# Products of P and values in two attention groups: column-tiled matmuls issued in larger runs

## The chip, the cores and the metric

The kernel runs on one core of a Trainium2 chip. The metric is the device time of one execution in microseconds (us). Times of runs are medians; the trace is one profiled execution.

## What is computed

The program is a two-layer backbone over 2048 latent tokens and 256 context tokens (2304 keys), width 1024. Each layer has four groups of heads that read one input projection, then one output projection. The change touches two groups:

```
# group A: 4 query heads, 2 key/value heads of width 64 (two query heads share one key/value head)
p = softmax(q @ k^T * 64**-0.5);  o = p @ v
# group B: 4 heads, two softmax maps over keys of width 32
p1 = softmax(q1 @ k1^T * 32**-0.5);  p2 = softmax(q2 @ k2^T * 32**-0.5)
o = (p1 - lam * p2) @ v;  then a norm per head
# group C: neighbourhood attention with bias, the same product p @ v with 6 or 7 key tiles
```

Group D is a state-space layer. Scores use a 32-bit type of reduced precision, and the products of P and values plain 32-bit floats, each of which the trace shows as two matmul records.

## The kernel before

Keys are cut into 18 tiles of 128 (16 latent, 2 context). Per layer the ten attention units run in the order of `UNITS` (a0, b0, a1, b1, c0, b2, c1, b3, c2, c3; `chain`, L1857). While one unit attends, the input projection of the next is woven into it as filler by `F.pe`, `F.act`, `F.dve` and `F.keys` (class `Fill`): one `F.pe(1)` puts a weight block's three matmuls (L377, L378, L379) there. The order on TensorE, ScalarE and VectorE is that of the code (`manual_schedule`); GpSimd and the DMA queues are ordered by the scheduler.

**Group A** (`attend_a`, L754). A unit is one key/value head with its two query heads. It goes over blocks of 512 queries (4, and one of 256 context queries in layer 0) and in each over the 18 key tiles x. `score(x)` (L873) puts the transposed scores of both query heads into one PSUM tile sx with four matmuls (L878, L879), and ScalarE's two exponentials (L881) write them as PT tiles. `value(x)` (L883) has two column-tiled matmuls (L886): the values are 128 keys by 64, so head 0 fills columns 0 to 63 of the array and head 1 columns 64 to 127, and both accumulate in one PSUM tile acc. `value` also adds PT into running sums (L897), on GpSimd for some tiles and on VectorE for the others. In step x the loop calls `value(x - 1)`. In between, `ahead` works out the row maxima of the next block in parts: a matmul L812 into sz or sy, a reduction L814 on VectorE. The last block of a unit has no next one, and filler may have run out.

**Group B** (`attend`, L954, `maps == 2`). A unit is one head, an iteration one tile of 128 queries, for i in three stages: scores (L1001) into sx, sz, sy of map 0 and map 1, maxima (L1045), exponentials (L1060), and for the tile before, the combined P (`combine`, L1084), its transposes (`trans`, L1100) in groups g = 0 to 4 of 4, 4, 4, 4 and 2 key tiles into one PSUM tile tr, `evac` (L1114) on ScalarE from tr to a PT tile, and `pv` (L1116) with one column-tiled matmul for each key tile (L1126): even key tiles on columns 0 to 63, odd ones on 64 to 127, the halves added later by `ysum` (L1137). There is one tr, so a `trans` waits for the `evac` of the group ahead of it. The order around the change, with filler left out:

```
first half:   pv 1 | scores map 1 part 0 | part 1 | evac 2, trans 3, evac 3 | part 2 | pv 2 | trans 4
              pv 3 | evac 4 | trans 0 of the next tile | pv 4
second half:  scores map 0 of the next tile, trans 1, ysum ... | pv 0 | trans 2
```

PT tiles come from a ring of 7, shared by the groups.

Of the kernel before, what the change touches and what calls it, by code (L numbers as in the profile page):

```python
# [9 lines left out]
F32 = mybir.dt.float32  # L10
# [148 lines left out]
class Net:  # L159
# [594 lines left out]
    def attend_a(self, l, G, F):  # L754
# [3 lines left out]
        nc, p = self.nc, self.ap  # L758
# [68 lines left out]
        def finish(ts, raw, tot):  # L827

            n = len(ts)
            rec = p.tile([128, 2, 4], F32, name="mxa")  # L830
            for h in range(2):
                lp = self.ps_tr(n * 128)
                for i in range(n):
                    nc.tensor.matmul(lp[:, i * 128:(i + 1) * 128], tot[:, h, i * 128:(i + 1) * 128], self.two,
                                     start=True, stop=True)
                nc.vector.reciprocal(rec[:, h, :n], lp.rearrange("p (n d) -> p n d", d=128)[:, :, 0])
                yield
            tr = self.ps_tr(n * 128)
            for i in range(n):
                nc.tensor.transpose(tr[:, i * 128:(i + 1) * 128], raw[:, 0, i * 128:(i + 1) * 128], self.ident)  # L840
            yo = raw[:, 1].rearrange("p (n d) -> p n d", d=128)
            for i in range(n):
                for h in range(2):
                    o = slice(h * 64, h * 64 + 64)
                    nc.vector.scalar_tensor_tensor(yo[:, i, o], tr[:, i * 128 + h * 64:i * 128 + h * 64 + 64],
                                                   rec[:, h, i:i + 1], gt[:, ts[i], o], op0=OP.mult, op1=OP.mult)
            for i, t in enumerate(ts):
                nc.sync.dma_start(self.y[l, t][:, G["col"]:G["col"] + 128], yo[:, i])
            yield
# [15 lines left out]
        for b, ts in enumerate(blocks):  # L865
            w = len(ts) * 128
            kts = list(range(NT)) if ts[0] < NLAT else [NLAT, NLAT + 1]
            n = len(kts)
            Q = Qs.pop(b)
            ahead = maxima(b + 1) if b + 1 < len(blocks) else iter(())  # L870
            sums, PTs, held = {}, {}, []

            def score(x):  # L873
                ks = slice(kts[x] * 128, kts[x] * 128 + 128)
                PTs[x] = [p.tile([128, 512], F32, name="PT", bufs=7) for _ in range(2)]
                o = self.ps_s(0, 1024)
                for h in range(2):
                    nc.tensor.matmul(o[:, h * 512:h * 512 + w], kst[:, ks], Q[0][:, h, :w], start=True, stop=False)  # L878
                    nc.tensor.matmul(o[:, h * 512:h * 512 + w], k2[0:65, ks], Q[1][0:65, h, :w], start=False, stop=True)  # L879
                for h in range(2):  # L880
                    nc.scalar.activation(PTs[x][h][:, :w], o[:, h * 512:h * 512 + w], AF.Exp, scale=0.125)  # L881

            def value(x):  # L883
                PT = PTs.pop(x)
                for h in range(2):
                    nc.tensor.matmul(acc[h * 64:(h + 1) * 64, :w], v[:, kts[x], :], PT[h][:, :w], start=(x == 0),  # L886
                                     stop=(x == n - 1))
                e = x // 2 if x < 4 else int(x % 3 == 2)
                if x in (0, 2):
                    held.append(PT)  # L890
                    return
                eng = nc.gpsimd if e else nc.vector
                if x in (1, 3):
                    sums[e] = p.tile([128, 2, 512], F32, name="Ta", bufs=3)
                for h in range(2):
                    first = held[e][h] if x in (1, 3) else sums[e][:, h]
                    eng.tensor_tensor(sums[e][:, h, :w], first[:, :w], PT[h][:, :w], op=OP.add)  # L897

            for x in range(n):
                F.t += 1  # L900
                score(x)
                if x % 4 == 2:
                    next(ahead, None)
                if x == 1:
                    acc = self.ps_acc()
                if 2 <= x <= 4:
                    next(done, None)
                if x:
                    value(x - 1)
                if x:  # L910
                    next(ahead, None)
                F.pe(1, 2)
                F.pe(1)
                if x:
                    next(ahead, None)
                F.act()
                if x % 2:
                    F.keys()
                if x % 2:
                    F.keys_copy()  # L920
                F.dve()
                yield True
            F.pe()
            value(n - 1)
            raw = p.tile([128, 2, 512], F32, name="Ta", bufs=3)
            nc.scalar.activation(raw[:, 0, :w], acc[:, :w], AF.Copy)
            for _ in done:
                F.pe(A_REST)
            for h in range(2 if n > 2 else 0):
                nc.vector.tensor_tensor(sums[0][:, h], sums[0][:, h], sums[1][:, h], op=OP.add)  # L930
            for _ in ahead:
                F.pe()
            done = finish(ts, raw, sums[0])
# [20 lines left out]
    def attend(self, l, G, F):  # L954


        nc, p = self.nc, self.ap
        kind, maps = G["kind"], G["maps"]
        steps = list(range(NT if l == 0 else NLAT))
        n = len(steps)  # L960
# [126 lines left out]
        def group(t, g):  # L1087
            kts = R[t, 0]["kts"]
            g0 = g * 4
            return kts[g0:g0 + 4], g0, len(kts)  # L1090
# [11 lines left out]
        def evac(t, g):  # L1102
            grp, g0, _ = group(t, g)
            if not grp:
                return
            r = R[t, 0]
            PT = r["PT", g] = p.tile([128, 4, 128], F32, name="PT", bufs=7)
            tr = r.pop(("tr", g))
            full = sum(1 for x in grp if x[2] == 128)
            spans = [(128, 0, full)] if full else []  # L1110
            if full < len(grp):
                spans.append((grp[-1][2], full, len(grp)))
            for w, x, y in spans:
                nc.scalar.activation(PT[:w, x:y], tr[:w, x * 128:y * 128].rearrange("p (a b) -> p a b", b=128), AF.Copy)  # L1114

# [43 lines left out]
        def at(i, f, *a):  # L1159
            if 0 <= i < n:  # L1160
                f(steps[i], *a)
# [5 lines left out]
        def half():  # L1167
            F.t += 1
            return True
# [10 lines left out]
        yield True  # L1180
        for i in range(n + (3 if maps == 2 else 2)):
            if maps == 2:
                at(i - 2, pv, 1)
                F.act()
                at(i, maxes, 0)
# [11 lines left out]
                if not early:  # L1197
                    at(i - 2, trans, 2)
                at(i - 2, evac, 2)
                at(i - 2, trans, 3)  # L1200
                at(i, exp, 0, 2)
                at(i - 2, evac, 3)
                at(i, scores, 1, 2)
                at(i - 2, pv, 2)
                at(i - 2, trans, 4)
                F.dve()
                F.pe(1)
                at(i - 3, finish)
                at(i, maxes, 1)
                at(i - 2, pv, 3)  # L1210
                F.act()
                F.pe(1)
                F.pe()
                F.act()
                early = i < n and not F.merged
                at(i - 2, evac, 4)
                F.act()
                if early:
                    at(i - 1, trans, 0)
                at(i - 2, pv, 4)  # L1220
                yield half()
                at(i, sums, 0)
                at(i, neg_max, 1)
# [26 lines left out]
                    F.keys(1)  # L1250
                    F.keys_copy()
                F.keys_copy()
                at(i - 1, pv, 0)
                early = i + 1 < n and not F.merged
                F.dve()
                if early:
# [747 lines left out]
```

## Time and profile before

| what | us |
|---|---|
| median of 3 runs (5153.1 to 5166.4) | 5156.62 |
| the profiled execution, its own time | 5158.76 |
| its span in the trace | 5156.9 |
| TensorE busy (matmuls) | 4681.1 (91%) |
| VectorE, ScalarE, GpSimd busy | 3215.5, 2568.4, 1912.5 |
| mean granted TensorE clock | 0.958 |

In the trace, PE is TensorE's matmuls, PEld its weight loads, DVE VectorE, ACT ScalarE, POOL GpSimd. A timeline row is a group of equal instructions: its start, the time to its end, engine, line, operation, out<-in, how many, and in brackets how long the engine was idle before it and what ended that. Matmuls are pipelined and their ends are modelled, so that rows overlap: what a group costs is read from one row's start to the start of the next. A "MATMUL ... x8" of L1126 is 4 key tiles.

### The profile page before, as it was taken

The page shows a single profiled execution, that of the slowest core. Times are in us where ns is not written, and L with a number is a line of the kernel's source. Part 1 is how long each engine was busy: PE and PEld are TensorE (multiplying, and loading weights), DVE is VectorE, ACT ScalarE, POOL GpSimd, SP SyncE. Part 2 cuts the span into 40 slices and gives each one's busy share as a digit, 9 for nine tenths or more (in the row PEclk, how much of TensorE's full clock was granted, in tenths as well). Part 3 has the DMA queues.
Part 4 walks back from the last instruction along what each step waited for, and adds up shares of the span by engine and source line. Part 5 has one row for each costly group of instructions (what it writes and reads, how often), then busy time and mean ns, then how long its engine had stood idle before and what let it go on. Part 6 is the DMA issues. An engine that isn't in the chain of part 4 may idle for free. (4 is left out here: it accounts for less than half of the span.)

```text
span 5156.9 us, 85866 instructions
## 1 busy us (share of the span) xinstructions
PE 4681.1 (91%) x31076; PEld 3585.3 (70%) x31076; DVE 3215.5 (62%) x7061; ACT 2568.4 (50%) x6522; POOL 1912.5 (37%) x3035
## 2 busy tenths in 40 slices
PE   7788998899999999998996879988999999999998
PEld 3686646665678777776676866566657777877777
DVE  8473767676674846724972737686767648476245
ACT  3332346634675856744341233466346658566431
POOL 4363443434233233321642534434342332333112
PEclk8899999999999999999998999999999999999999
DMA  7847212322235344253668573123223343433432
GB/s 255 287 151 202 88 41 66 98 95 72 91 121 167 103 144 132 83 178 116 194 213 281 169 198 109 49 65 98 95 72 98 111 152 100 155 122 117 130 134 107
DMA packets 360184, 677.66 MB, mean 131 GB/s; under 512 B 161872, under 2 KB 262224, under 8 KB 306768
## 3 DMA queue, kind: packets, MB, share of 16 engines
q0 software_dynamic: 54432, 396.39, 22.9%
q1 hardware_dynamic: 299280, 270.47, 17.9%
q10 hardware_dynamic: 6048, 5.31, 0.3%
q8 instruction: 247, 4.05, 0.3%
q14 instruction: 177, 1.45, 0.1%
HBM read 561.66 MB, written 110.36 MB: 130 GB/s over the span
## 5 line engine op out<-in xcount | busy, mean ns | idle before, releaser
L377 PE MATMUL pj<-WH,hs 128*128 128x256 f32 (+2 forms) x2592 | 814.9, 314 | 22.1 <-ACT b_v L733 7.1
L378 PE MATMUL pj<-WL,hs 128*128 128x256 f32 (+2 forms) x2592 | 753.3, 291 | 2.7 <-POOL WL L367 2.7
L379 PE MATMUL pj<-WH,hs 128*128 128x256 f32 (+2 forms) x2592 | 752.3, 290 | 0.0
L1114 ACT ACTIVATE PT<-tr 128x512 f32<-128x512 f32 (+1 forms) x788 | 440.5, 559 | 310.0 <-PE tr L1100 303.3
L377 PEld LDWEIGHTS pj<-WH,hs 128*128 128x128 f32 x2592 | 498.1, 192 | 125.3 <-issue 68.2
L388 POOL DMA_DIRECT2D hs<-hs x378 | 227.7, 603 | 956.0 <-PE pj L379 475.6
L378 PEld LDWEIGHTS pj<-WL,hs 128*128 128x128 f32 x2592 | 499.2, 193 | 26.6 <-POOL WL L367 3.3
L881 ACT ACTIVATE PT<-sx 128x512 f32<-128x512 f32 x584 | 315.3, 592 | 378.1 <-PE sx L879 367.6
L379 PEld LDWEIGHTS pj<-WH,hs 128*128 128x128 f32 x2592 | 497.7, 192 | 2.4 <-issue 2.4
L1045 DVE TENSOR_REDUCE sm<-sx 128x1 f32<-128x1024 f32 (+1 forms) x276 | 321.8, 1166 | 210.2 <-PE sx L1001 208.9
L1060 ACT ACTIVATE Ta<-sx,sm 128x1024 f32<-128x1024 f32 (+1 forms) x340 | 324.5, 955 | 108.2 <-DVE sm L1054 87.2
L886 PE MATMUL acc<-PT,a_v 128*64 128x512 f32 (+1 forms) x1168 | 315.8, 617 | 0.0
L897 POOL TENSOR_TENSOR Ta<-Ta,PT 128x512 f32<-128x512 f32 x160 | 219.5, 1389 | 204.4 <-ACT PT L881 203.9
L1126 PE MATMUL acc<-PT,b_v 128*64 128x128 f32 (+1 forms) x3200 | 277.9, 290 | 4.4 <-DVE sm L1073 1.5
L1001 PE MATMUL sx<-b_kst,qs 128*128 128x512 f32 (+2 forms) x618 | 218.3, 441 | 58.1 <-ACT Ta L1060 57.4
L814 DVE TENSOR_REDUCE mxa<-sy 128x1 f32<-128x1024 f32 (+1 forms) x256 | 209.8, 820 | 89.9 <-PE sy L812 86.8
L897 DVE TENSOR_TENSOR Ta<-Ta,PT 128x512 f32<-128x512 f32 x288 | 217.0, 794 | 77.0 <-ACT PT L881 76.5
L878 PE MATMUL sx<-Tb,a_kst 128*128 128x512 f32 x584 | 246.8, 423 | 19.5 <-ACT PT L881 19.5
L1100 PE MATMUL tr<-ident,Ta 128*128 128x128 f32 x1576 | 246.5, 278 | 13.9 <-ACT PT L1114 10.2
L1045 DVE TENSOR_REDUCE sm<-sy 128x1 f32<-128x768 f32 (+1 forms) x260 | 245.4, 944 | 15.7 <-PE sy L1001 14.4
L814 DVE TENSOR_REDUCE mxa<-sz 128x1 f32<-128x512 f32 x256 | 175.5, 686 | 123.5 <-PE sz L812 121.7
L377 PE MATMUL s<-WH,hs 128*128 128x256 f32 (+1 forms) x576 | 193.4, 337 | 44.9 <-DMA hs<-hs 20.7
(388 smaller groups left out, 12175.2 us busy)
## 6 DMA issues: line engine op xcount, KB each, us to landing
hs<-hs POOLq DMA_DIRECT2D x378, 1024.0 KB, 5.2
hs<-hs SPq DMA_DIRECT2D x36, 1024.0 KB, 4.8
hs<-in_w_ada SPq DMA_DIRECT2D x48, 512.0 KB, 4.5
wst<-in_w_in SPq DMA_DIRECT2D x576, 32.0 KB, 1.9
yin<-y SPq DMA_DIRECT2D x30, 512.0 KB, 4.0
h<-in_xT SPq DMA_DIRECT2D x18, 512.0 KB, 6.6
U<-ud SPq DMA_DIRECT2D x64, 144.0 KB, 3.6
x<-zn SPq DMA_DIRECT2D x18, 512.0 KB, 2.7
```

Of the source, the lines that this page charges most:

```text
L377: nc.tensor.matmul(ps, H[:, k, :], WH[k][:, c0:c1], start=(k == 0), stop=False)
L378: nc.tensor.matmul(ps, H[:, k, :], WL[k][:, c0:c1], start=False, stop=False)
L379: nc.tensor.matmul(ps, L[:, k, :], WH[k][:, c0:c1], start=False, stop=(k == NK - 1))
L814: nc.vector.tensor_reduce(nm if one else mx[:, j:j + 1], s, axis=AX.X, op=OP.max, negate=one)
L878: nc.tensor.matmul(o[:, h * 512:h * 512 + w], kst[:, ks], Q[0][:, h, :w], start=True, stop=False)
L881: nc.scalar.activation(PTs[x][h][:, :w], o[:, h * 512:h * 512 + w], AF.Exp, scale=0.125)
L886: nc.tensor.matmul(acc[h * 64:(h + 1) * 64, :w], v[:, kts[x], :], PT[h][:, :w], start=(x == 0), stop=(x == n - 1))
L897: eng.tensor_tensor(sums[e][:, h, :w], first[:, :w], PT[h][:, :w], op=OP.add)
L1045: nc.vector.tensor_reduce(mx[:, j:j + 1] if len(tiles) > 1 else nm, s, axis=AX.X, op=OP.max, negate=len(tiles) == 1)
L1060: nc.scalar.activation(r["P"](a, b), src, AF.Exp, bias=r["sm"][:, 5:6], accum_out=r["sm"][:, 6 + j:7 + j])
L1114: nc.scalar.activation(PT[:w, x:y], tr[:w, x * 128:y * 128].rearrange("p (a b) -> p a b", b=128), AF.Copy)
L1126: nc.tensor.matmul(acc[t][half * 64:half * 64 + 64, :], G["v"][:w, kt, :], PT[:w, j, :], start=(x < 2), stop=x >= nkt - 2)
```

## The change

In group A a step with even x (from 2 on) calls `value(x - 2)` and `value(x - 1)`, a step with odd x none, and the block's end the last two. In group B `pv 0` goes from the end of the second half to the start of the next, right ahead of `pv 1`, and `pv 2` and `pv 3` go behind `trans 0`, right ahead of `pv 4`. The PT ring has 8 tiles. No instruction is added or left out.

```diff
@@ attend_a
-                PTs[x] = [p.tile([128, 512], F32, name="PT", bufs=7) for _ in range(2)]
+                PTs[x] = [p.tile([128, 512], F32, name="PT", bufs=8) for _ in range(2)]
...
-                if x:
+                if x and x % 2 == 0:
+                    value(x - 2)
                     value(x - 1)
...
             F.pe()
+            value(n - 2)
             value(n - 1)
@@ attend
-            PT = r["PT", g] = p.tile([128, 4, 128], F32, name="PT", bufs=7)
+            PT = r["PT", g] = p.tile([128, 4, 128], F32, name="PT", bufs=8)
...
             if maps == 2:
+                at(i - 2, pv, 0)
                 at(i - 2, pv, 1)
...
                 at(i, scores, 1, 2)
-                at(i - 2, pv, 2)
                 at(i - 2, trans, 4)
                 F.dve()
                 F.pe(1)
                 at(i - 3, finish)
                 at(i, maxes, 1)
-                at(i - 2, pv, 3)
...
                 if early:
                     at(i - 1, trans, 0)
-                at(i - 2, pv, 4)
+                for g in (2, 3, 4):
+                    at(i - 2, pv, g)
                 yield half()
...
-                at(i - 1, pv, 0)
                 early = i + 1 < n and not F.merged
```

What it does to TensorE's order is shown at three places. In the changed kernel the lines of `attend` stand 2 further down (L1100 is L1102, L1126 is L1128, L1001 is L1003). Place 1, group B, TensorE, end of the first half; tr is the transposes' PSUM tile, a_gt here holds the values of head b2. Before:

```order
L1100 MATMUL tr<-ident,Tb 128x128 x4
L1001 MATMUL sy<-b_kst,qs 128x512
L1001 MATMUL sy<-b_kst,qs 128x256
L1126 MATMUL acc<-PT,a_gt 64x128 x4
L1100 MATMUL tr<-ident,Tb 128x128 x2
L377 MATMUL pj<-WH_17367,hs 128x256
L378 MATMUL pj<-WL_17369,hs 128x256
L379 MATMUL pj<-WH_17367,hs 128x256
L1126 MATMUL acc<-PT,a_gt 64x128 x4
```

In the changed kernel:

```order
L1102 MATMUL tr<-ident,Tb 128x128 x4
L1003 MATMUL sy<-b_kst,qs 128x512
L1003 MATMUL sy<-b_kst,qs 128x256
L1102 MATMUL tr<-ident,Tb 128x128 x2
L377 MATMUL pj<-WH_17367,hs 128x256
L378 MATMUL pj<-WL_17369,hs 128x256
L379 MATMUL pj<-WH_17367,hs 128x256
L377 MATMUL pj<-WH_17388,hs 128x256
L378 MATMUL pj<-WL_17390,hs 128x256
L379 MATMUL pj<-WH_17388,hs 128x256
L1102 MATMUL tr<-ident,Ta 128x128 x4
L1128 MATMUL acc<-PT,a_gt 64x128 x10
```

Between the 4 and the 2 transposes (`trans 3`, `trans 4`) the 4 products are gone; they and those of `pv 3` stand behind the next tile's first transposes, 10 in a row. Place 2, group B, TensorE, start of the first half. Before:

```order
L379 MATMUL pj<-WH_17483,hs 128x256
L1126 MATMUL acc<-PT,a_gt 64x128 x4
L1100 MATMUL tr<-ident,Tb 128x128 x4
L1126 MATMUL acc<-PT,a_gt 64x128 x4
L1001 MATMUL sx<-b_kst,qs 128x512 x2
```

In the changed kernel:

```order
L379 MATMUL pj<-WH_17508,hs 128x256
L1102 MATMUL tr<-ident,Tb 128x128 x4
L1128 MATMUL acc<-PT,a_gt 64x128 x8
L1003 MATMUL sx<-b_kst,qs 128x512 x2
L377 MATMUL pj<-WH_17521,hs 128x256
```

`trans 2` comes first, then `pv 0` and `pv 1` as 8 in a row. Place 3, group A, TensorE, an even and the odd step behind it, as pieces of the difference:

```order
 L812 MATMUL sz<-a_kst,Tb 128x512
 L794 MATMUL tr<-ident,xl 65x128 x2
-L886 MATMUL acc<-PT,a_v 64x512 x2
+L886 MATMUL acc<-PT,a_v 64x512 x4
 L812 MATMUL sy<-a_kst,Tb 128x256
```

```order
 L878 MATMUL sx<-Tb,a_kst 128x512
 L879 MATMUL sx<-Tb,a_k_2928 128x512
-L886 MATMUL acc<-PT,a_v 64x512 x2
 L812 MATMUL sy<-a_kst,Tb 128x512 x2
 L377 MATMUL pj<-WH_4838,hs 128x256
```

The odd step loses its two products and the even step has four. Over the program the runs of products of group B go from 633 to 256 and those of group A from 286 to 146; ScalarE's order of attention work stays as it was, on VectorE only the adds of L897 move with `value` (4 in a row where neither tile is GpSimd's), and on GpSimd some loads of hs (L388) now stand ahead of a pair of adds.

## Rows read from the trace of the kernel before

**Rows 1.** The page, busy time of TensorE in 40 equal slices of the span

```profile
PE   7788998899999999998996879988999999999998
```

**Rows 2.** Stretches: us, busy of PE, PEld, DVE, ACT, POOL, granted clock, DMA share, GB/s

```profile
740.00:763.00 23.00, 21.07 (x77) 8.05 (x76) 8.33 (x13) 10.86 (x20) 8.49 (x7) 1.00 0.00 1
785.00:803.00 18.00, 10.34 (x28) 7.44 (x29) 13.00 (x23) 9.65 (x23) 2.22 (x5) 0.53 0.03 8
```

**Rows 3.** PE's timeline, head b2 of layer 0, one first half

```profile
1702.21 0.73 PE L1001 MATMUL sx<-b_kst,qs 128*128 128x512 f32 x2
...
1703.72 0.60 PE L1100 MATMUL tr<-ident,Tb 128*128 128x128 f32 x4
...
1705.19 0.44 PE L1100 MATMUL tr<-ident,Tb 128*128 128x128 f32 x2
...
1705.71 0.28 PE L379 MATMUL pj<-WH,hs 128*128 128x256 f32 x1
1705.92 0.66 PE L1126 MATMUL acc<-PT,a_gt 128*64 128x128 f32 x8
1706.51 0.39 PE L377 MATMUL pj<-WH,hs 128*128 128x256 f32 x1
1706.73 0.28 PE L378 MATMUL pj<-WL,hs 128*128 128x256 f32 x1
1706.85 0.28 PE L379 MATMUL pj<-WH,hs 128*128 128x256 f32 x1
```

**Rows 4.** PE's timeline, head c0 of layer 1: a run of six products

```profile
4113.41 0.88 PE L1126 MATMUL acc<-PT,a_q 128*64 128x128 f32 x12
4114.21 0.39 PE L377 MATMUL pj<-WH,hs 128*128 128x256 f32 x1
```

**Rows 5.** ACT in the timeline, same half as rows 3

```profile
1700.46 1.12 ACT L1060 ACTIVATE Ta<-sx,sm 128x1024 f32<-128x1024 f32 x1 [0.22 <-DVE sm L1054]
...
1704.35 0.60 ACT L1114 ACTIVATE PT<-tr 128x512 f32<-128x512 f32 x1 [0.65 <-PE tr L1100]
```

**Rows 6.** PE's timeline, end of head b0, trans 3 and trans 4

```profile
1002.14 0.60 PE L1100 MATMUL tr<-ident,Tb 128*128 128x128 f32 x4
...
1003.42 0.44 PE L1100 MATMUL tr<-ident,Tb 128*128 128x128 f32 x2
```

**Rows 7.** ACT in the timeline, same place as rows 6

```profile
1002.77 0.60 ACT L1114 ACTIVATE PT<-tr 128x512 f32<-128x512 f32 x1 [1.79 <-PE tr L1100]
```

**Rows 8.** Waits in head b0, 810 to 985: us in total, times, longest

```profile
PEld sx L1001 <- ACT Ta L1060: 5.5, 14, 0.5
```

**Rows 9.** PE's timeline, head a0, steps x = 5 (543.01) and 11 (565.36)

```profile
543.01 0.48 PE L878 MATMUL sx<-Tb,a_kst 128*128 128x512 f32 x1
...
544.13 1.08 PE L886 MATMUL acc<-PT,a_v 128*64 128x512 f32 x4
545.14 0.39 PE L812 MATMUL sy<-a_kst,Tb 128*128 128x256 f32 x1
...
545.95 0.39 PE L878 MATMUL sx<-Tb,a_kst 128*128 128x512 f32 x1
...
565.36 0.39 PE L878 MATMUL sx<-Tb,a_kst 128*128 128x512 f32 x1
...
569.06 0.48 PE L878 MATMUL sx<-Tb,a_kst 128*128 128x512 f32 x1
```

**Rows 10.** The timeline, last block of a0, two whole steps

```profile
750.96 0.50 PE L878 MATMUL sx<-Tb,a_kst 128*128 128x512 f32 x1 [0.17 <-ACT PT L881]
...
752.21 1.09 ACT L881 ACTIVATE PT<-sx 128x512 f32<-128x512 f32 x2 [1.30 <-PE sx L879]
...
753.34 0.50 PE L878 MATMUL sx<-Tb,a_kst 128*128 128x512 f32 x1 [0.17 <-ACT PT L881]
...
755.79 0.50 PE L878 MATMUL sx<-Tb,a_kst 128*128 128x512 f32 x1 [0.23 <-ACT PT L881]
```

**Rows 11.** The page, group of VectorE's adds in group A: busy us, mean ns

```profile
L897 DVE TENSOR_TENSOR Ta<-Ta,PT 128x512 f32<-128x512 f32 x288 | 217.0, 794 | 77.0 <-ACT PT L881 76.5
```

## The prediction

> **What bounds the kernel now.** The page first: TensorE's slices stand at 9 tenths through nearly all of the attention [rows 1], so work taken off TensorE there shortens the run, as long as nothing else then ends last. Next the timeline of one group of products in group B, read from start to start. The group of 8 records (4 key tiles) in the middle of plain matmuls [rows 3] begins 0.21 after the matmul ahead of it (1705.71 to 1705.92), where two plain ones of this size are 0.12 apart (1706.73 to 1706.85); it lasts 0.59 to the next start (1706.51); and the plain matmul after it is again followed late, by 0.22 instead of 0.12. So a group that stands alone costs 0.09 + 0.59 + 0.10 = 0.78 us. A run of 12 records takes 0.80 [rows 4], 0.21 more than 8 do, so that 8 records added to a run cost 0.42 to 0.44; I take 0.44. **Joining a group to another is worth 0.78 - 0.44 = 0.34 us**, and 0.29 by my reading where transposes follow, which come late after any change of weights. In group A a tile's four records of 512 columns take 1.01 to the next start (544.13 to 545.14) [rows 9], with about 0.2 at their edges as in B, so 1.21; joined to another four they cost four times the columns of B's, about 0.86 (an estimate from 0.44 for eight). That saves 0.35 as well.
>
> With 377 runs joined in B and 140 in A all of it would be near 177 us. The question is what waits in the place of the time given back.
>
> **Group B, heads b1 to b3.** Four terms for an iteration.
> - `pv 0` joins `pv 1`: -0.29. The next work is the scores of map 1, which need the exponential over sx to be done: it ends at 1700.46 + 1.12 = 1701.58 [rows 5], and the scores start at 1702.21 [rows 3]. Where TensorE does wait for ScalarE it starts 0.05 after it (below), so 0.58 of room covers 0.29.
> - `pv 2` leaves its place between `trans 3` and `trans 4`: not 0.78. `trans 4` writes the one tile tr, which `evac 3` must have read. From the start of `trans 3` to that of `trans 4` it is 1.47 now (1703.72 to 1705.19) [rows 3], and ScalarE's copy, idle 0.65 for the transposes, ends at 1704.95 [rows 5]. At the end of b0 nothing but that copy sets the distance: 1.28 [rows 6], `trans 4` 0.05 behind the copy's end at 1003.37 [rows 7]. Of `pv 2`'s time 0.19 comes back; the other 0.59 turns into a wait of TensorE for ScalarE. Bounds: 0.19 and 0.78; I take 0.19, since both ends of that chain are in the rows; the 0.59 between them is the first rival's.
> - `pv 3` leaves a place between plain matmuls: -0.78. It covered nothing: `evac 4` is covered by the filler that stays.
> - Both join `pv 4`: 2 x 0.44 = +0.87.
>
> Together -0.29 - 0.19 - 0.78 + 0.87 = **-0.39**. The output sum (`ysum`) sees its last product at the same place as before. I count 67 of the 102 iterations of these six heads (three a layer, 18 and 16 tiles) in which TensorE is full and the filler runs; the others are the ends of a unit, where the unit behind is mixed in or filler is missing. 67 x 0.39 = 26 us.
>
> **Head b0.** Here the scores of map 1 already wait for the exponential in every iteration: 14 waits in 175 us [rows 8]. The first term is gone, -0.10 remains; 28 iterations in two layers, 3 us. The ends of the units I cost at nothing, between -3 (runs joined there too) and +10 us (where filler is missing `pv 3` covered the wait for `evac 4`).
>
> **Group A.** One PSUM tile sx serves all scores, so a step cannot be shorter than scores, two exponentials and the way back. In the last block, where neither maxima nor filler stand in between, TensorE waits in every step, and a step takes 753.34 - 750.96 = 2.38, the next 2.45 [rows 10]; I take 2.42. An odd step without its products falls to its own work: 2.94 - 1.21 = 1.73 for x = 5, 3.70 - 1.21 = 2.49 for x = 11 [rows 9]. The long one stays over 2.42 and its pair of steps gains 0.35; the short one waits 0.69, and its pair loses 0.34.
> - The ten blocks of a unit's first three that have maxima and filler throughout: 8 pairs x 0.35 = 2.8, less three short odd steps at about 0.6, plus 0.35 for the last two tiles at the end: -1.3 each, -13 us.
> - The last blocks of the four units: a pair takes 2 x 2.42 now; then 2.42 for the odd step and 0.95 + 1.21 + 0.86 = 3.02 for the even one (scores alone take 0.95, the 543.01 to 544.13 of rows 9 less the edge of the group behind them), +0.60 a pair, some +5 a block. Where a little filler is left it is less: +16 us over the four.
> - The two blocks in between, whose filler ends half way: nothing.
>
> Sum +3 us, with -20 (no waits in odd steps) and +15 (below) as bounds. The adds of L897 that now come four in a row hold VectorE for 4 x 0.79 = 3.2 [rows 11]; the reductions behind them free sz and sy, of which TensorE has two parts in hand, about a step of 3 to 4 us, so I cost this at nothing; were that room gone, it is up to a microsecond in two pairs of a block, the +15. GpSimd's loads of hs that now stand ahead of adds issue no more than before; an add may be late by two steps before its PT tile is wanted again, and the eighth tile gives that. It costs nothing, and the other queues carry nothing that moved. The odd and even order on TensorE is as the rows of place 3 show it, so I give no chance to the case that the change does not reach the chip.
>
> **The sum.** -26 - 3 + 3 = -26. Against the profiled execution: 5158.8 - 26 = 5133. That execution stands 2 us over the median of its runs, so I forecast a median of **5131 us**, with 5115 to 5148 as this case's own range, which takes in part of the bounds (A at -20 gives 5108, A at +15 and the unit ends at +10 give 5153). The rivals are given by the median too.
>
> **Rivals.**
> - *Every change of weights saved comes back.* The terms for `pv 2` and the odd steps would then be wrong, because something else fills their waits. B: 0.29 + 0.78 + 0.78 - 0.87 = 0.98 an iteration, 67 times, 66 us, and A 140 x 0.35 = 49 us: 5042 us. For it: the edges of a lone group are real [rows 3]. Against it: TensorE takes its work in order, and the waits that open have their floors in rows 6, 7 and 10. The Trainium skill (TensorEngine Tiling (Array Packing), Key Properties) says that a change of tiling mode drains TensorE. By that rule alone each of the 517 joined runs pays; the edges in rows 3 agree with a drain, the floors say that it is not all the rule needs. Chance 0.08.
> - *It evens out.* In b1 to b3 the waits of b0 appear too (the scores' room of 0.58 is used up by whatever ScalarE does first), which leaves -0.10 an iteration, 10 us, and A pays +8, between its +3 and +15: 5155 us. For it: in b0 this is the state already [rows 8]. Chance 0.22.
> - *Slower: the clock falls in the bare blocks of group A.* In an odd step there TensorE would work 0.95 of 2.42 us, where it now works 2.16. With 21.07 of 23 us busy the granted clock was 1.00; where it was busy 10.34 of 18 us it was 0.53, the 1.2 GHz level [rows 2]. At that level the 0.95 of an odd step's scores and the 3.02 of an even step double, +4 us a pair less what the floor hides, some 3.5 us x 8 pairs x 2 wholly bare blocks = 56 us: 5187 us. It decides whether the clock falls there at all: the rows have it in full while every step is 2.16 of work and a short wait, and have no block whose steps are by turns 0.95 and 3.02. The Trainium skill (TensorE: Matmul & The Clock Gate, A second HAM failure mode: psum-queue depth-cycling) tells of a kernel whose short idle times between groups of matmuls, one group a bank, made the clock swing; by it this rival holds, while no row here shows a fall in a block of group A that steps at its floor. Chance 0.07.
>
> **How the numbers follow.** Forecast 0.63, rivals 0.08, 0.22 and 0.07. A measurement of this kernel tells about 0.3% from no change, 15.5 us: below 5141.1 is faster, above 5172.1 slower. Faster: 0.56 of the forecast's 0.63 and the first rival, 0.64. Slower: the last rival and the upper edge of the second, 0.08. Same: 0.28. The range 5104 to 5163 holds the forecast, most of the second rival and the space between the forecast and the first, 8 times in 10.
>
> **What would show it.** In heads b1 to b3 of the new profile: runs of 16 and 20 records of L1128; 1.28 to 1.30 from `trans 3` to `trans 4`, with a new wait of TensorE for ScalarE's L1116 of about 0.6 in each iteration; and the distance from one `trans 4` to the next shorter by 0.39. In b0 periods nearly as before. In the last blocks of group A pairs of 2.4 and 3.0, in the others odd steps of no less than 2.4. Wrong would be: a shorter distance from `trans 3` to `trans 4` (then the first rival), a granted clock below 1 in the last blocks of a0 (the third), waits of TensorE for L814 behind four adds, or a period of b1 to b3 that did not move (the second).

## The result and the profile after

The changed kernel takes **5213.74 us** (median of 4 runs), the kernel before 5157.31 beside it: a ratio of 1.0106, 95% interval 1.0089 to 1.0124. It is slower by 56 us where 26 less were forecast, and lies outside both of the forecast's ranges. The profiled execution has a span of 5213.1 us at a mean granted clock of 0.950, where before it was 5156.9 at 0.958. One of the six executions of e7, further down, took 14846 us; its ratio leaves that one out.

On TensorE only the products stand elsewhere, so the starts of all other matmuls can be laid side by side. Read so, from one profiled execution of each kernel, the sixteen full blocks of group A take **76.7 us longer** together (each one by 0.3 to 11.2), and group B's stretches take some 16 us less.

**As forecast** was the pair of steps. An odd and an even one in a covered block, one that has maxima and filler, on TensorE: the start of the step behind them before, then both in the changed kernel (columns as in [rows 9]):

```profile
572.35 0.39 PE L878 MATMUL sx<-Tb,a_kst 128*128 128x512 f32 x1
```

```profile
565.12 0.39 PE L878 MATMUL sx<-Tb,a_kst 128*128 128x512 f32 x1
...
567.60 0.47 PE L878 MATMUL sx<-Tb,a_kst 128*128 128x512 f32 x1
...
568.71 1.94 PE L886 MATMUL acc<-PT,a_v 128*64 128x512 f32 x8
...
571.74 0.39 PE L878 MATMUL sx<-Tb,a_kst 128*128 128x512 f32 x1
```

The odd step, 3.70 before [rows 9], takes 2.48; the even one, 3.29 before (569.06 [rows 9] to 572.35), takes 4.14. That is -1.22 and +0.85, the forecast's 1.21 and 0.86: where nothing else ends last, a joined pair gains its 0.35.

**Not as forecast** were the waits. TensorE's waits in layer 0's a0, b0 and a1 (us in total, times, longest), before over 526 to 1357 us and after over 523 to 1390:

```profile
PE sx L878 <- ACT PT L881: 10.4, 27, 1.2
...
PE sz L812 <- DVE mxa L814: 1.2, 4, 0.4
```

```profile
PE sx L878 <- ACT PT L881: 25.5, 35, 1.2
PE sz L812 <- DVE mxa L814: 20.2, 19, 2.5
```

The first row grows by the short odd steps that end at the exponentials' floor, which the forecast had. The second was priced at nothing: 19 us more here, 21 more in layer 1. One of these waits, on TensorE, VectorE and GpSimd:

```profile
552.10 0.50 PE L812 MATMUL sz<-a_kst,Tb 128*128 128x512 f32 x1
...
553.37 0.28 PE L812 MATMUL sy<-a_kst,Tb 128*128 128x256 f32 x1
553.49 0.40 PE L878 MATMUL sx<-Tb,a_kst 128*128 128x512 f32 x1
...
557.11 0.47 PE L812 MATMUL sz<-a_kst,Tb 128*128 128x512 f32 x1 [2.51 <-DVE mxa L814]
...
559.59 0.78 PE L878 MATMUL sx<-Tb,a_kst 128*128 128x512 f32 x1
```

```profile
549.38 1.23 DVE L814 TENSOR_REDUCE mxa<-sy 128x1 f32<-128x1024 f32 x1 [0.49 <-PE sy L812]
...
552.42 3.94 DVE L897 TENSOR_TENSOR Ta<-Ta,PT 128x512 f32<-128x512 f32 x4
556.28 0.68 DVE L814 TENSOR_REDUCE mxa<-sz 128x1 f32<-128x512 f32 x1
```

```profile
553.37 1.72 POOL L897 TENSOR_TENSOR Ta<-Ta,PT 128x512 f32<-128x512 f32 x1
```

The reduction of the last sz stands behind four adds, which end at 556.3; TensorE has filler, its scores and one part of maxima to do and then waits 2.5 us. The first three blocks of the four units have two such fours each, and TensorE waits behind every one of the 24, for 0.9 to 2.5 us, 39 us in all. What follows is the second cost. The stretches of that wait and behind it, and then an odd, an even and the next even step of a bare block (columns as in [rows 2]):

```profile
553.49:557.11 3.62, 1.11 (x7) 0.60 (x5) 3.62 (x5) 1.09 (x2) 3.62 (x4) 1.00 0.08 18
558.24:561.64 3.40, 3.40 (x12) 2.71 (x11) 1.80 (x2) 0.60 (x1) 0.60 (x1) 0.50 0.40 140
```

```profile
759.91:762.36 2.45, 1.22 (x6) 0.67 (x4) 0.51 (x1) 1.08 (x2) 0.00 (x0) 1.00 0.00 0
762.36:766.98 4.62, 4.62 (x13) 1.51 (x13) 2.08 (x4) 1.08 (x2) 0.00 (x0) 0.63 0.01 2
...
769.35:772.34 2.99, 2.99 (x12) 1.16 (x13) 1.07 (x2) 1.08 (x2) 2.12 (x2) 1.00 0.00 0
```

After TensorE was busy 1.11 of 3.62 us the granted clock stands at half, the 1.2 GHz level, for 3.4 us, and the step that began at 553.49 takes 6.10 where it took 4.81. The clock falls so behind 11 of the 24 waits. In the bare block (the last full one of a unit, where maxima and filler are all but gone) the even steps take 3.0 at the full clock, as forecast, but some of them fall to 0.63 and take 4.6. Counted as time at the low level times one half, group A's blocks lose 46 us more to the clock than before. That is an upper bound, since some of it lies beside waits.

**Group B**, head b2: `trans 4` (x2) and `trans 0` of the next tile (x4, from Ta) before, then the same with a full iteration in the changed kernel, TensorE and then ScalarE (columns as in [rows 3, 5]):

```profile
1728.70 0.44 PE L1100 MATMUL tr<-ident,Tb 128*128 128x128 f32 x2
...
1730.84 0.60 PE L1100 MATMUL tr<-ident,Ta 128*128 128x128 f32 x4
...
1739.91 0.44 PE L1100 MATMUL tr<-ident,Tb 128*128 128x128 f32 x2
...
1741.69 0.60 PE L1100 MATMUL tr<-ident,Ta 128*128 128x128 f32 x4
...
1751.00 0.44 PE L1100 MATMUL tr<-ident,Tb 128*128 128x128 f32 x2
```

```profile
1757.29 0.44 PE L1102 MATMUL tr<-ident,Tb 128*128 128x128 f32 x2 [0.21 <-ACT PT L1116]
...
1758.64 0.60 PE L1102 MATMUL tr<-ident,Ta 128*128 128x128 f32 x4
...
1764.27 0.66 PE L1102 MATMUL tr<-ident,Tb 128*128 128x128 f32 x4
1764.85 1.09 PE L1128 MATMUL acc<-PT,a_gt 128*64 128x128 f32 x16
...
1767.03 0.60 PE L1102 MATMUL tr<-ident,Tb 128*128 128x128 f32 x4
...
1768.31 0.44 PE L1102 MATMUL tr<-ident,Tb 128*128 128x128 f32 x2 [0.29 <-ACT PT L1116]
1768.93 0.39 PE L377 MATMUL pj<-WH,hs 128*128 128x256 f32 x1 [0.17 <-ACT b_v L733]
...
1769.75 0.60 PE L1102 MATMUL tr<-ident,Ta 128*128 128x128 f32 x4
1770.28 1.31 PE L1128 MATMUL acc<-PT,a_gt 128*64 128x128 f32 x20
...
1779.40 0.44 PE L1102 MATMUL tr<-ident,Tb 128*128 128x128 f32 x2 [0.30 <-ACT PT L1116]
```

```profile
1763.62 0.60 ACT L993 ACTIVATE qs<-tr 128x512 fp32r<-128x512 f32 x1 [0.16 <-PE tr L991]
...
1768.58 0.30 ACT L733 ACTIVATE b_v<-pj 128x128 f32<-128x128 f32 x1
```

The runs of 16 and 20 are there, and `trans 3` to `trans 4` is 1.28 (1767.03 to 1768.31), as forecast. Two more waits are there, in every second iteration each. `trans 2` starts 0.05 after the copy L993 of the new queries out of the tile tr (1763.62 + 0.60, then 1764.27), where `pv 0` used to stand in between. And the filler (L377) comes 0.62 after `trans 4`, 0.05 behind the copy L733 that empties its tile pj; without that wait it is 0.20. From one `trans 4` to the next the distance was 11.21 and 11.08 or 11.09 in turn and is 11.03 (1757.29 to 1768.31, rounded) and 11.09: -0.085 an iteration on the mean, not -0.39.

### The profile page after: what moved, and what is told of

It is laid out like the page before. It is cut to its first block, busy times and chain, and to the rows that moved or that the text cites. A ratio compares the mean times of both kernels' runs of the same rounds, so it can differ in the third digit from the quotient of the medians.

```text
span 5213.1 us, 85887 instructions
## 1 busy us (share of the span) xinstructions
PE 4623.0 (89%) x31076; PEld 3636.7 (70%) x31076; DVE 3261.6 (63%) x7061; ACT 2570.0 (49%) x6522; POOL 1934.5 (37%) x3035
## 5 line engine op out<-in xcount | busy, mean ns | idle before, releaser
L377 PE MATMUL pj<-WH,hs 128*128 128x256 f32 (+2 forms) x2592 | 806.2, 311 | 27.7 <-ACT b_v L733 9.1
L377 PEld LDWEIGHTS pj<-WH,hs 128*128 128x128 f32 x2592 | 500.5, 193 | 98.1 <-issue 31.7
L1116 ACT ACTIVATE PT<-tr 128x512 f32<-128x512 f32 (+1 forms) x788 | 440.5, 559 | 257.4 <-PE tr L1102 253.5
L388 POOL DMA_DIRECT2D hs<-hs x378 | 227.4, 602 | 915.8 <-PE pj L379 483.8
L881 ACT ACTIVATE PT<-sx 128x512 f32<-128x512 f32 x584 | 315.4, 592 | 459.1 <-PE sx L879 456.2
L1062 ACT ACTIVATE Ta<-sx,sm 128x1024 f32<-128x1024 f32 (+1 forms) x340 | 325.0, 956 | 128.9 <-DVE sm L1056 109.5
L897 DVE TENSOR_TENSOR Ta<-Ta,PT 128x512 f32<-128x512 f32 x288 | 255.9, 935 | 103.2 <-ACT PT L881 103.2
L897 POOL TENSOR_TENSOR Ta<-Ta,PT 128x512 f32<-128x512 f32 x160 | 218.3, 1379 | 228.0 <-ACT PT L881 227.6
L886 PE MATMUL acc<-PT,a_v 128*64 128x512 f32 (+1 forms) x1168 | 298.6, 630 | 0.0
L1102 PE MATMUL tr<-ident,Tb 128*128 128x128 f32 x1280 | 216.2, 284 | 59.1 <-ACT PT L1116 48.6
L814 DVE TENSOR_REDUCE mxa<-sy 128x1 f32<-128x1024 f32 (+1 forms) x256 | 209.6, 819 | 92.8 <-PE sy L812 91.6
L1003 PE MATMUL sx<-b_kst,qs 128*128 128x512 f32 (+2 forms) x618 | 219.2, 442 | 51.9 <-ACT Ta L1062 49.8
L1102 PE MATMUL tr<-ident,Ta 128*128 128x128 f32 x1576 | 246.2, 278 | 18.2 <-ACT PT L1116 14.4
L814 DVE TENSOR_REDUCE mxa<-sz 128x1 f32<-128x512 f32 x256 | 175.2, 684 | 105.2 <-PE sz L812 103.1
L1128 PE MATMUL acc<-PT,b_v 128*64 128x128 f32 (+1 forms) x3200 | 235.4, 283 | 4.4 <-DVE sm L1075 1.5
```

Source lines behind the costliest of these rows:

```text
L377: nc.tensor.matmul(ps, H[:, k, :], WH[k][:, c0:c1], start=(k == 0), stop=False)
L814: nc.vector.tensor_reduce(nm if one else mx[:, j:j + 1], s, axis=AX.X, op=OP.max, negate=one)
L1003: nc.tensor.matmul(s[:, o0:o0 + w], lt, r["ks"][:, k0:k0 + w], start=(x == 0), stop=(x == len(r["ops"]) - 1))
L1062: nc.scalar.activation(r["P"](a, b), src, AF.Exp, bias=r["sm"][:, 5:6], accum_out=r["sm"][:, 6 + j:7 + j])
L1102: nc.tensor.transpose(tr[:w, j * 128:(j + 1) * 128], r["P"](c, c + w), self.ident)
L1128: nc.tensor.matmul(acc[t][half * 64:half * 64 + 64, :], G["v"][:w, kt, :], PT[:w, j, :], start=(x < 2), stop=x >= nkt - 2)
```

## The experiments

Ratios are to the kernel before, run beside it on the same chip, in five rounds.

| run | median, us | ratio | 95% interval |
|---|---|---|---|
| e1_a_alone | 5228.1 | 1.0128 | 1.0113 to 1.0144 |
| e2_b_alone | 5142.4 | 0.9966 | 0.9954 to 0.9977 |
| e3_a_adds_apart | 5190.7 | 1.0055 | 1.0042 to 1.0067 |
| e4_b_keep_pv2 | 5124.0 | 0.9928 | 0.9916 to 0.9941 |
| e5_adds_in_fours | 5206.7 | 1.0087 | 1.0065 to 1.0109 |
| e6_filled_odd_steps | 5178.2 | 1.0037 | 1.0024 to 1.0050 |
| e7_joined_where_it_pays | 5105.6 | 0.9896 | 0.9871 to 0.9920 |
| e8_b_pv01_alone | 5137.1 | 0.9953 | 0.9934 to 0.9971 |

**Each half alone.** e1 is the diff without its hunks in group B's loop, e2 the diff without those in `attend_a`; both have the eight PT tiles.

> Group A's part of the change alone (B's order as before). Theory 1, the loss is all group A's: its sixteen blocks took 76.7 us longer in the changed kernel, the rest of the program some 19 less; so this kernel should take 5157 + 76 = 5225 to 5237 us, with waits of TensorE's sz for the maxima (L814) of some 40 us in all and a granted clock of half in the same steps. Rival, the two parts hurt one another (the PT ring of a unit that ends in the merged stage, GpSimd's order): alone A stays within 5145 to 5185.

> Group B's part alone (A as before). Theory 1: it gains what its stretches show in the changed kernel, 0.08 us an iteration of b1 to b3 and 0.06 of b0, with the ends of the units 13 to 19 us: 5138 to 5144 us. Rival, as predicted before the result, -0.39 an iteration, which group A's uneven steps took away: 5124 to 5133 us.

e1: +66 us (1.28% of 5157), its sixteen blocks 72.3 longer, 43 us of TensorE's waits of sz for L814. e2: -17.5 us. The halves add up to +48, with 6 to 8 us of uncertainty in each, against the +55 of the whole change by its ratio; within that no part of the loss needs both. Theory 1 holds.

**The adds back at their places, and the adds alone moved.** e3 takes the adds out of `value` into `add` and issues them where they stood; e5 leaves the products at one tile a step and puts only the adds in fours (the adds are on line 900 there). The loop's lines against the kernel before; the block's end is left out:

```
 e3:                                   e5:
+    if x and x % 2 == 0:                   if x:
+        value(x - 2)                           value(x - 1)
+        value(x - 1)                  +    if x and x % 2 == 0:
     if x:                             +        add(x - 2)
-        value(x - 1)                  +        add(x - 1)
+        add(x - 1)
```

> Group A's products joined by two, but the adds (L897) of each key tile issued at the step where they stood before, two at a time, and B as before. Theory 1, the four adds in a row hold VectorE, the maxima wait behind them, TensorE waits for sz and the clock falls after that: the 40 us of waits for L814 go, and with them the low clock in the blocks that have maxima (24 us of lost clock), so group A stands at +77 - 64 = +13 and the kernel at 5163 to 5175 us. Rival, the uneven steps themselves do it wherever the adds stand (short odd steps end at the exponentials' floor, the even ones run at a low clock): 5215 to 5235 us.

> Group A's products stay one tile a step, as before, and only the adds (L897) of two tiles are issued together, in even steps; B as before. Theory 1, four adds in a row are by themselves what delays the maxima, and through them TensorE's sz, and the clock falls after that idle time: waits of TensorE for L814 of 30 to 42 us, 48 us in all (72.3 - 24.4 between the two kernels that differ in the adds' place alone): 5190 to 5215 us. Rival, four adds hurt only where the short odd steps have taken the room away: 5153 to 5175 us.

The waits of e3 and of e5 over 520 to 1390 us:

```profile
PE sx L878 <- ACT PT L881: 26.5, 39, 1.2
...
PE sz L812 <- DVE mxa L814: 1.8, 6, 0.4
```

```profile
PE sz L812 <- DVE mxa L814: 20.5, 17, 2.4
```

e5, in which no product has moved, takes 45 us more (0.87%), with 41 us of waits for L814 over both layers: four adds in a row do it alone. e3, in which every product is joined, has these waits out, and in the eight first and second blocks of the units the low clock too; these are now 1.2 to 1.7 us shorter than before, where the forecast said 1.3. As a whole e3 takes 28 us more than before and lies in neither expected range. Its blocks stand at +24.4 and not at the +13 expected, because the last blocks are 5.5 to 9.4 longer and the four third ones 7 together, nearly all of it lost to the clock. What lowers the clock in the third blocks no run shows.

**The clock of the bare blocks.** e6 is e3 with work put into the waits:

```
+    if x % 2 and x >= 5 and n > 2 and ts[0] >= 12:
+        o = self.ps_s(1, 512)
+        for _ in range(3):
+            nc.tensor.matmul(o[:, :w], kst[:, 0:128], Q[0][:, 0, :w], start=True, stop=True)
```

> As e3_a_adds_apart, with three more matmuls of 512 columns in the odd steps of group A's last full block from the sixth tile on, into a PSUM tile that nothing reads: work put into TensorE's wait. Theory 1, the clock falls there because TensorE idles 1.2 of 2.4 us in every odd step, and 0.7 us of work hides in the wait: more work, less time, the low clock in the last blocks of the four units (13.7 us lost in e3, of which the kernel before lost 1.7) goes to 0 to 5 us: 8 to 13 us under e3, 5177 to 5183 us; the pairs still take 2.4 and 3.0. Rival, the clock falls for another reason (the runs of eight products, or only the idle time at a block's end): same as e3 or up to 6 us longer, 5186 to 5197 us.

The last block of a0 in layer 0 before, in the changed kernel, in e3 and in e6, from its first scores to those behind it (columns as in [rows 2]):

```profile
720.32:768.81 48.49, 43.70 (x177) 19.93 (x177) 18.88 (x37) 21.67 (x41) 16.80 (x17) 1.00 0.02 6
```

```profile
728.19:786.56 58.37, 48.20 (x177) 23.11 (x177) 18.82 (x37) 21.56 (x41) 16.76 (x17) 0.88 0.02 5
```

```profile
715.85:769.85 54.00, 43.82 (x178) 20.98 (x177) 18.77 (x37) 21.55 (x41) 16.75 (x17) 0.97 0.02 5
```

```profile
721.17:773.77 52.60, 46.65 (x199) 24.62 (x198) 19.12 (x37) 21.56 (x41) 17.11 (x17) 1.00 0.02 5
```

21 more matmuls, and the block is 1.4 us shorter, at the full clock throughout; its pairs take 2.4 and 3.0. One block alone would prove little, since one fall of the clock is worth 1.7 us and blocks with the same code differ by as much between runs (54.4 us before and 53.2 in e2, the last block of a1 in layer 0). But all four last blocks are shorter, by 0.7 to 3.4 us. The last whole odd and even step of this block in e3 and in e6:

```profile
759.30:761.75 2.45, 1.22 (x6) 0.68 (x4) 0.51 (x1) 1.08 (x2) 1.49 (x2) 1.00 0.00 0
761.75:766.45 4.70, 4.70 (x12) 1.40 (x12) 2.08 (x4) 1.09 (x2) 0.00 (x0) 0.64 0.00 0
```

```profile
764.61:767.06 2.45, 1.92 (x10) 1.25 (x8) 0.51 (x1) 1.09 (x2) 1.49 (x2) 1.00 0.00 0
767.06:770.07 3.01, 3.01 (x13) 1.17 (x13) 1.92 (x4) 1.09 (x2) 0.00 (x0) 1.00 0.00 0
```

From x = 5 on seven even steps of the four last blocks fall like this in the changed kernel, six in e3 and none in e6. The clock loss of the four falls from 15.4 to 6.8 us, and nearly all that is left lies in the third step (x = 2), behind an odd step that was not filled. By the ratios the kernel is 9 us faster than e3, with as much uncertainty. The runs of eight products are still there, so the rival is out: what pulled the clock down was the idle half of the odd step.

**Group B in parts.** e8 joins `pv 0` to `pv 1` and nothing else; e4 also joins `pv 3` to `pv 4` and leaves `pv 2` where it was. The lines of e4 against the kernel before:

```
+                at(i - 2, pv, 0)
                 at(i - 2, pv, 1)
...
                 at(i - 2, pv, 2)
                 at(i - 2, trans, 4)
...
-                at(i - 2, pv, 3)
...
-                at(i - 2, pv, 4)
+                for g in (3, 4):
+                    at(i - 2, pv, g)
...
-                at(i - 1, pv, 0)
```

> Group B with pv 0 joined to pv 1 and nothing else changed. Theory 1: -0.11 and -0.37 in turn, as the changed kernel's stretches show from trans 0's side to the scores of map 1: -0.24 an iteration, 67 times, -16 us, nothing in b0: ratio 0.996 to 0.998, and the distance of two trans 4 at 11.1 and 10.7. Rival, the shorter part is filled up by a later wait, of trans 4 for evac 3 or the scores for the exponentials: 0.9985 to 1.001. The difference to e4 is what moving pv 3 alone brings: -0.13 an iteration by theory 1, -0.35 by the prediction.

> Group B with pv 0 joined to pv 1 and pv 3 to pv 4, but pv 2 left where it covers the wait of trans 4 for evac 3; A as before. Theory 1, each of the terms as the changed kernel's stretches show it: pv 0 -0.11 and -0.37 in turn, pv 3 -0.79 and -0.34 in turn (in every second iteration TensorE's filler then waits 0.42 for ScalarE's copy L733, which pv 3 used to cover), joined +0.43: -0.38 an iteration, 67 times, -25 us, with up to -9 from b0: 5123 to 5133 us. Rival, ScalarE or VectorE set the iteration and any time that TensorE saves turns into another wait: 5137 to 5145 us, as with all of B's part.

e4, head b2, one iteration from `trans 4` to `trans 4`:

```profile
1747.27 0.44 PE L1100 MATMUL tr<-ident,Tb 128*128 128x128 f32 x2
...
1749.01 0.88 PE L1126 MATMUL acc<-PT,a_gt 128*64 128x128 f32 x12
...
1754.02 1.09 PE L1126 MATMUL acc<-PT,a_gt 128*64 128x128 f32 x16
...
1757.44 0.66 PE L1126 MATMUL acc<-PT,a_gt 128*64 128x128 f32 x8
1758.03 0.44 PE L1100 MATMUL tr<-ident,Tb 128*128 128x128 f32 x2
```

It takes 10.76, 0.38 less than the mean of before, and the kernel is 0.72% faster, some 37 us, 20 more than with `pv 2` joined as well. e8's distances are 11.15 and 10.78, 0.18 less on the mean, which makes 12 us in 67 iterations. Its 0.47% are 24 us (15 to 34 by the interval), more than this and than was expected; where the rest lies no run settles. From e8 to e4, `pv 3` brings 0.2 an iteration, between the 0.13 of theory 1 and the 0.35.

**Joined where it pays.** e7 is e4 with group A's products joined, adds at their old steps, in the first two blocks of a unit and only in some pairs:

```
+            def pair(x):
+                return b < 2 and x in (4, 8, 10, 12, 14, 16, 18)
```

> As e4_b_keep_pv2, and group A's products joined, with the adds at their old steps, only in the first two blocks of a unit and only in the pairs whose odd step stays over the exponentials' floor or nearly so (x = 4, 8, 10, 12, 14, 16 and the last pair). Theory 1, the pairs of e3 add up: -2.0 and -1.9 in a block, 8 blocks, -16 us on top of e4's -38 against the kernel before: ratio 0.988 to 0.991. Rival, the room is gone once B is shorter or the adds' order is mixed: 0.992 to 0.995, as e4.

Its eight blocks are 1.8 to 2.0 us shorter each, 15 us together, and the ratio is **0.9896**: some 54 us faster than before and 108 faster than the change as it stood. Theory 1 had 0.988 to 0.991.

## Why the prediction was wrong

- **The prices of a group** were right: 0.35 for a joined pair of group A, 0.87 for two groups added to a run of B.
- **The floors** were right: odd steps end at 2.3 to 2.5 us, bare pairs take 2.4 and 3.0, `trans 3` to `trans 4` takes 1.28. Taken by themselves group A's steps cost what was forecast: e3's blocks are 24.4 us longer, of which up to 20.5 is the clock, which leaves +4 or more where the sum had +3. By kinds of block this is -12 for the eight first and second ones, nothing for the third and +15 for the last, where the forecast had -13 (for ten blocks), nothing and +16. e6 gives the same sum, 16.4 less 11.9.
- **The step that failed is "the adds of L897 that now come four in a row ... so I cost this at nothing"**, with +15 for all of group A as its upper bound. From e3 to e1 these adds are worth 38 us by the ratios (give or take 10) and 48 by the blocks, in e5 45. Two things were wrong. The room was not two parts and a step of 3 to 4 us: in the rows of that wait TensorE has work for 2.5 us from its last matmul into sz (552.10) to the start of the wait (557.11 less 2.51), with one part in hand. It is not the joined products that took this room, for in e5, where the steps have kept their length, TensorE waits up to 2.4 us at the same places. And VectorE is held for longer than 3.2: the 24 fours take 3.9 to 4.9, since an add next to GpSimd's is slower (last section), and in that wait 3.0 us of other work without a pause (from 549.38) stand ahead of them.
- **The third rival happened in part.** Its mechanism, the clock in the bare blocks, is what e6 shows, at 22 us more of lost clock in the last blocks here (14 in e3) instead of 56, because it fell in the third step of each block and in seven even steps behind it, not in every pair, and a fallen even step takes 4.6, not twice 3.0; it was given 0.07. The clock also fell in covered blocks, behind the waits for L814, a place that no rival named. The Trainium skill (TensorE: Matmul & The Clock Gate, A second HAM failure mode: psum-queue depth-cycling) tells of short idle times between groups of matmuls that make the clock swing; the even steps of a0's last block at 4.6 and 3.0 us, and at 3.0 throughout from x = 6 in e6, agree with it.
- **The second rival's number came out for B, not its mechanism.** It had -0.10 an iteration, near the -0.085, by waits of the scores for the exponentials. These are 0.5 us in all over six iterations (1757 to 1823, weight loads of L1003 for L1062); the waits that took the gain are those for the copies L1116, L733 and L993.
- **`pv 3` "covered nothing"** was wrong. In every second iteration it covered ScalarE's copy L733, for which the filler's tile pj waits: from `trans 4` to `trans 0` 0.79 came back in one iteration and 0.34 in the next (2.14 to 1.35, 1.78 to 1.44), where 0.78 was counted in each. Joining it cost the forecast 0.43, so that it was worth 0.14 on the mean by these stretches and 0.2 by e4 against e8, not 0.35.
- **`pv 0`** gave 0.11 and 0.37 in turn, not 0.29 (0.06 and 0.30 in e8, by itself). Its room was checked against the exponential alone; in iterations that prepare new queries it also covered the copy L993, which `trans 2` waits for.
- **`pv 2`** gave its 0.19 as forecast. It should not have been moved at all for that: it costs 0.43 in the run, and e4, which leaves it, is 20 us faster than e2. Each term had been worked out, but not each term's own balance.
- **The sum for B**: -0.24 - 0.18 - 0.565 + 0.87 = -0.115 by these parts, -0.085 measured. 67 times that is 6 us and b0 another 2, with 0.06 an iteration where 0.10 was forecast. e2's 17.5 us, with 6 of uncertainty, leave some 10 for the ends of the units, costed at nothing.
- **The PT ring** cost nothing, as forecast: over the whole run ScalarE's waits for a PT tile (L881 for L897) fall from 9.1 to 1.5 us. For GpSimd's loads no run shows the cost by itself.
- **Added up**, forecast and result are 82 us apart: 38 to 48 for the adds, up to 20 for the clock where e3 shows it without them, 20 for group B's iterations, less the 10 at the ends of its units. That makes 68 to 78; the rest is within the uncertainty of the ratios.

What is not settled is how much of the adds' cost is their standing in a row and how much their slowness beside GpSimd: during every one of the 24 fours GpSimd works for over two thirds of the time, in e5 too. An upper bound for the slowness, estimated from the rows of the 24, is 30 of the 39 us of waits: for each the time that it takes over 3.2, as far as its wait goes.

## What to carry to other kernels

An instruction that stands alone at a dear place may be the cover of several waits, each in its own iteration; before it is moved, the next use of every tile around it has to be checked against the engine that empties it, in even and odd iterations apart. Joining work makes the steps uneven: the short step is bound by what was hidden before, and whatever travels with the joined work (here the adds) arrives as a burst on another engine, so it should be moved apart. Join only where the step that gives the work away stays over its floor: e7 has the gain of the pairs without their cost.

## What had not been expected of the hardware

VectorE's add of L897 takes longer beside GpSimd's work. Four of them, and what GpSimd does meanwhile, in the changed kernel:

```profile
575.89 4.91 DVE L897 TENSOR_TENSOR Ta<-Ta,PT 128x512 f32<-128x512 f32 x4
```

```profile
576.17 3.22 POOL L897 TENSOR_TENSOR Ta<-Ta,PT 128x512 f32<-128x512 f32 x2 [0.76 <-ACT PT L881]
579.35 0.90 POOL L541 TENSOR_TENSOR pe<-pe,sub 128x128 f32<-128x128 f32 x1
```

That is 1.2 us each. Over the whole run of the changed kernel the add takes 0.68 with no GpSimd arithmetic beside it (129 of them) and 1.25 where GpSimd works over half of its time (122). In fours the adds fall together with GpSimd's more often than before, and the mean goes from 794 ns [rows 11] to 935:

```profile
L897 DVE TENSOR_TENSOR Ta<-Ta,PT 128x512 f32<-128x512 f32 x288 | 255.9, 935 | 103.2 <-ACT PT L881 103.2
```

The Trainium skill (SBUF — State Buffer, Who interferes with whom) says that a VectorE instruction with two SBUF inputs contends with a GpSimd instruction that reads SBUF; these rows agree.

The other surprise is that 21 matmuls whose result nobody reads make a block shorter (52.60 us for 54.00, and the other three last blocks with it), since the clock that they hold up is worth more than they take.
